# A value step one unit later, and cached keys prepared during the projection before: the attention of a two-layer decoder step on one core

## The chip, the core and the metric

The kernel runs on one core of a Trainium2 chip. Its time is the device time of one execution, in microseconds. The core has five engines that run on their own and wait for each other by semaphores: TensorE (PE, matmuls and transposes by matmul; the loading of its weights is shown apart as PEld), VectorE (DVE), ScalarE (ACT), GpSimd (POOL) and SyncE (SP). SP, ACT and POOL issue DMA transfers, each from its own queue, in the order of its program.

## The reference: what is computed

One inference step of a decoder with two layers, for a prompt of 512 tokens and for 8 single tokens, each with a cache of 128 keys and values. All is in float32. In outline, with D_MODEL 1024, 16 heads of 64, 4 key/value heads, D_FF 2816:

```python
x = x + 0.5 * swiglu(rms(x))            # layer 0
x = x + pool_mixer(rms(x))
x = x + 0.5 * swiglu(rms(x))
k, v = split(rms(x) @ w_kv); k = rope(k)      # one shared K and V
x = x + 0.5 * swiglu(rms(x))            # layer 1, the "down projection" ends this
q = rope(rms(x) @ w_q)
s = q k^T / 8, masked to a causal window of 128
m = maximum(max(s), sink); p = exp(s - m)
o = (p / (sum(p) + exp(sink - m))) @ v
x = x + o @ w_o
x = x + 0.5 * swiglu(rms(x))
y = rms(x)
```

For a single token the keys are its 127 latest cached keys and the new one, and the values likewise. Further outputs are the last 128 keys and values and the last rows of the pooling mixer.

## The kernel before

**Layout and precision.** The residual stream lies transposed in eight tiles `x[k]` of 128 channels by 520 tokens (512 of the prompt, 8 single). A float32 product is made of three fast matmuls: each operand is split into a rounded part and the rest (`split`, lines 238 to 246: ACT copies the rounded part, L242; DVE subtracts, L243), and hi x hi, lo x hi and hi x lo are summed (`terms`, `mm`). Weights are split in the same way by `Weights._split` (L191 on ACT, L192 on DVE).

**Weights.** The class `Weights` streams weight chunks from memory to `raw` buffers (three of 1 MB) on SP's queue and keeps five split pieces ahead of their use. A chunk's load waits until the pieces of the chunk that had its buffer are split. `later` keeps these issues in the order in which they are written. The order of the other instructions on each engine is made by a scheduler when the program is built; pools of buffers (`raw`, `S`, `xh`, `tl`, four PSUM pairs of banks by `duo` and `ps`) decide what has to wait for what.

**Down projection.** `ffn(2, ...)` is the feed-forward half step ahead of the attention. Its last part computes eight tiles, each with matmuls at L410, an eviction by DVE into `u` and an addition to `x[m]` (L589, L590), and then `deferred`, which makes the next layer's split input. A generator given as `before_last` is advanced once per tile.

**Attention.** The queries are eight tiles of two heads. `q_part(t, h)` does one half of tile `t` (24 matmuls at L410), `q_evac` its rotary embedding and split. A unit is a query tile and two of the four blocks of 128 tokens, so there are 16 units. A unit goes through

- `scores` (twelve matmuls, L1004 to L1006),
- `softmax` (mask and maximum on DVE, L1019; exponentials on ACT, L1034; scaling by the sum, half on ACT, L1040, half on DVE, L1042),
- `turn` (transposes by PE, L1052, then `split`),
- `values` (twelve matmuls, L1075, and two copies to `oT` on ACT, L1087).

The loop at line 1211 runs over iterations n: scores of unit n, turn of unit n - 2 (`LAG`), query halves, jobs, softmax of unit n, values of unit n - 2.

**Single tokens.** `turn_keys(b)` transposes the cached keys of token b in iterations 0 to 7 (L1120, copied back by L1121). `sample_scores` (L1127) runs in iterations 10 and 11, `sample_softmax` in 11, `sample_values` (L1159) in 13, all sixteen matmuls at a stretch; the profile shows each of them as two. The caches come on ACT's queue (L950, L953), and the new keys and values are written over row 0 of them by POOL's queue (L951, L954).

**Output projection.** `o_part(m, k0)` adds four of eight input tiles to output tile `m`. The first halves run in iterations 12 to 17 as `jobs`, the second ones after the loop.

Of the kernel before, what the change touches and what calls it, by code (L numbers as in the profile page):

```python
# [18 lines left out]
P = 128  # L19
# [8 lines left out]
PARTS = (8, 8, 6)  # L28
LAG = 2
NPL = (3, 2, 2, 2)  # L30
HD = 64
# [178 lines left out]
def yoco_step(ctx, tc, ins, outs):  # L210
# [651 lines left out]
    with ff_pool() as tmp:  # L862
# [47 lines left out]
        def outputs():  # L910
# [21 lines left out]
            nc.gpsimd.dma_start(v_win_s[:, 127].rearrange("b g d -> b (g d)"), vnew)  # L932

        step = lambda: next(steps, None)
# [6 lines left out]
    with tc.tile_pool(name="at", bufs=2) as at:  # L941
        cst = at.tile([P, 512], F32, name="cst", bufs=1)
        nc.scalar.dma_start(cst, consts[:, C_MASK : C_MASK + 512])
        cosq, sinq = pair(XX, [P, TOK], F32)
        nc.scalar.dma_start(cosq, consts[:, C_COS : C_COS + TOK])
        nc.scalar.dma_start(sinq, consts[:, C_SIN : C_SIN + TOK])
# [3 lines left out]
        nc.scalar.dma_start(kc, cache_k.rearrange("b s g d -> s b (g d)"))  # L950
        nc.gpsimd.dma_start(kc[0:1], knew)  # L951
        for i in range(4):
            nc.scalar.dma_start(vc[i], cache_v[2 * i : 2 * i + 2].rearrange("b s g d -> s b (g d)"))  # L953
            nc.gpsimd.dma_start(vc[i][0:1], vnew[2 * i : 2 * i + 2, :])  # L954

# [3 lines left out]
        oT = [big.tile([P, SP], F32, tag="th", name="oT") for t in range(KT)]  # L959
        kk, vv = [], []  # L960
        for g in range(2):
            kk.append(pair(("tl", "tl"), [P, SP]))
            split(kk[g], kT[g][:, :SP])
        for b2 in range(2):
            vv.append(pair(("tl", "tl"), [P, 2, 256]))
            split(vv[b2], vtok[:, 2 * b2 : 2 * b2 + 2, :])

        def q_half(banks, k0):
# [138 lines left out]
        qq[0] = q_evac(0, qb[0])  # L1107
        q_parts = {1: [(3, 0), (3, 1)]}
        q_evacs = {0: 1, 1: 2, 2: 3}
# [5 lines left out]

        def turn_keys(b):

            pk = ps()
            for g in range(2):
                T.transpose(pk[:, g * P : (g + 1) * P], kc[:, b, g * P : (g + 1) * P], ident)  # L1120
            S.copy(kc[:, b, :], pk[:, :256])  # L1121

        def sample_scores(pd, bs):
            for b in bs:
                for g in range(2):
                    c0 = b * 16 + g * 8
                    T.matmul(  # L1127
                        pd[:, 0, c0 : c0 + 8],
                        kc[:, b, g * P : (g + 1) * P],
                        qz[:, g, :, :, b],  # L1130
                        start=True,
                        stop=True,
                    )

        def sample_softmax(pd):

            sT = at.tile([P, P], F32, name="sT", bufs=1)
            V.tensor_copy(sT, pd[:, 0, :P])
            T.transpose(pd[:, 1, :P], sT, ident)
            smx = at.tile([P, 4], F32, name="smx", bufs=1)  # L1140
            pr = at.tile([P, P], F32, name="pr", bufs=1)
            V.tensor_reduce(smx[:, 0:1], pd[:, 1, :P], axis=AX.X, op=ALU.max)
            V.scalar_tensor_tensor(smx[:, 1:2], smx[:, 0:1], -1.0, sink_s[:, 1:2], op0=ALU.mult, op1=ALU.min)
            S.activation(pr, pd[:, 1, :P], AF.Exp, bias=smx[:, 1:2], accum_out=smx[:, 2:3])
# [6 lines left out]
        def sample_values(pd, pr, bs):  # L1151
            if bs[0] == 0:
                T.transpose(pd[:, 0, :P], pr, ident)
                V.tensor_copy(prT, pd[:, 0, :P])
            pO = pd[:, 1, :P]
            for b in bs:
                for g in range(2):
                    c0 = b * 16 + g * 8
                    T.matmul(  # L1159
                        pO[:, c0 : c0 + 8],  # L1160
                        vc[b // 2][:, b % 2, g * P : (g + 1) * P],
                        prT[:, c0 : c0 + 8],
                        start=True,
                        stop=True,
                    )
            if bs[-1] < NS - 1:
                return
            pO5 = pO.rearrange("p (b t e i) -> p e t i b", b=NS, t=2, e=2)
            for e in range(2):
                rows = slice(e * 64, e * 64 + 64)  # L1170
                for g in range(2):
                    V.tensor_copy(oS[rows, g * 4 : g * 4 + 4, :], pO5[rows, e, g, :, :])

# [11 lines left out]
        def o_part(m, k0, halves_=(0, 1), after=None):  # L1185
# [12 lines left out]

        pd_s, pd_v = [], []
# [121 lines left out]
```

## Time and profile before

| | |
|---|---|
| median of 3 runs | 1728.08 us (1722.71 to 1731.19) |
| profiled execution | 1729.8 us |
| its span, first to last instruction | 1728.0 us |
| instructions | 34367 |
| PE busy | 1669.6 us, 97% |
| DVE busy | 1269.1 us, 73% |
| ACT busy | 904.7 us, 52% |
| mean granted PE clock | 0.980 |

The span is one profiled execution, the time around it is 1.8 us. "Busy" is the time in which an engine executes; matmuls overlap in the array, so a busy PE need not be at its peak. PEclk is the clock that PE was granted, as a share of the full one. In rows of instructions, `out<-in` are the program's tile names, and what stands behind an arrow is the instruction that ended a wait.

### The profile page before, as it was taken

What the parts mean: (1) busy time and instruction counts of PE and PEld (TensorE: products, weight loads), DVE (VectorE), ACT (ScalarE), POOL (GpSimd) and SP (SyncE); (2) the same over time, 40 slices, a digit from 0 to 9 for tenths busy, and PEclk for the clock granted to TensorE, in tenths of its full rate; (3) what the DMA queues carried; (4) which work ended last, traced back from release to release, by engine and by line L of the source; (5) the groups of instructions that cost most, each with busy time, mean ns of one, the idle gap of its engine ahead of it and who ended that gap; (6) DMA issues with size and microseconds to landing.
All of it is one profiled execution on the core that took longest, in us unless ns stands there. A gap on an engine that the chain in (4) does not pass through costs nothing.

```text
span 1728.0 us, 34367 instructions
## 1 busy us (share of the span) xinstructions
PE 1669.6 (97%) x13701; PEld 1654.0 (96%) x13701; DVE 1269.1 (73%) x2454; ACT 904.7 (52%) x1810; POOL 146.1 (8%) x178
## 2 busy tenths in 40 slices
PE   7999999999899999999999999998889999999996
PEld 7999999999899999999999999998779899999996
DVE  6966866877875875887866866878756785785765
ACT  6643634656552643655543634647855653462553
POOL 0101101001001101001101101100000110110100
PEclk9999999999999999999999999999979999999998
DMA  8646746663445845546646746642112465666531
GB/s 204 159 129 141 171 135 144 180 183 75 102 141 132 182 134 135 141 128 145 155 127 141 174 135 141 155 140 50 25 35 73 111 163 144 146 150 159 135 86 51
DMA packets 315872, 227.06 MB, mean 131 GB/s; under 512 B 9265, under 2 KB 290969, under 8 KB 315671
## 3 DMA queue, kind: packets, MB, share of 16 engines
q1 hardware_dynamic: 285872, 174.82, 35.5%
q0 software_dynamic: 23200, 41.82, 14.7%
q10 hardware_dynamic: 6638, 8.23, 1.5%
q8 instruction: 107, 1.75, 0.4%
q14 instruction: 55, 0.44, 0.1%
HBM read 180.89 MB, written 5.04 MB: 108 GB/s over the span
## 4 chain that ended last, share of the span: by engine, by line
PE 67%; DVE 4%; ACT 3%; issue 0%; ACTq 0%; DVEq 0%
PE ps L435 35%; PE ps L410 30%; ACT sm L1034 1%; DVE sm L1019 1%; PE ps L1075 1%; DVE wl L192 1%; PE ps L1159 0%; PE ps L1052 0%; DVE xl L243 0%; ACT xh L242 0%; PE ps L1127 0%; DVE rp L856 0%; ACT wh L191 0%; PE ps L1250 0%; ACT oT L1087 0%
## 5 line engine op out<-in xcount | busy, mean ns | idle before, releaser
L191 ACT ACTIVATE wh<-raw 128x512 fp32r<-128x512 f32 (+1 forms) x742 | 449.6, 621 | 542.8 <-PE ps L410 326.3
L192 DVE TENSOR_TENSOR wl<-raw,wh 128x512 fp32r<-128x512 f32 (+1 forms) x742 | 491.0, 677 | 206.9 <-ACT wh L191 202.2
L435 PE MATMUL ps<-th,wh 128*128 128x260 f32 x1264 | 358.4, 284 | 5.4 <-ACT th L242 3.7
L435 PE MATMUL ps<-tl,wh 128*128 128x260 f32 x1264 | 358.7, 284 | 0.4 <-DVE tl L243 0.4
L435 PE MATMUL ps<-th,wl 128*128 128x260 f32 x1264 | 356.5, 283 | 0.6 <-DVE wl L192 0.5
L410 PE MATMUL ps<-hh,wh 128*128 128x260 f32 x1376 | 282.1, 286 | 4.0 <-DVE mx L1019 3.0
L410 PE MATMUL ps<-hl,wh 128*128 128x260 f32 x1376 | 280.9, 284 | 0.0
L410 PE MATMUL ps<-hh,wl 128*128 128x260 f32 x1376 | 279.4, 283 | 0.0
L435 PEld LDWEIGHTS ps<-th,wh 128*128 128x128 f32 x1264 | 238.9, 189 | 6.7 <-ACT th L242 4.1
L435 PEld LDWEIGHTS ps<-tl,wh 128*128 128x128 f32 x1264 | 239.4, 189 | 1.3 <-DVE tl L243 1.3
L435 PEld LDWEIGHTS ps<-th,wl 128*128 128x128 f32 x1264 | 238.6, 189 | 1.0 <-DVE wl L192 1.0
L410 PEld LDWEIGHTS ps<-hh,wh 128*128 128x128 f32 x1376 | 213.4, 190 | 5.4 <-DVE mx L1019 3.6
L410 PEld LDWEIGHTS ps<-hl,wh 128*128 128x128 f32 x1376 | 215.0, 190 | 0.0
L410 PEld LDWEIGHTS ps<-hh,wl 128*128 128x128 f32 x1376 | 214.0, 189 | 0.0
L435 PE MATMUL ps<-xh,wh 128*128 128x260 f32 x708 | 198.9, 283 | 0.6 <-ACT wh L191 0.6
L435 PE MATMUL ps<-xl,wh 128*128 128x260 f32 x708 | 198.6, 283 | 0.0
L435 PE MATMUL ps<-xh,wl 128*128 128x260 f32 x708 | 194.7, 282 | 1.0 <-DVE wl L192 1.0
L156 POOL DMA_DIRECT2D raw<-raw x79 | 68.4, 866 | 1389.1 <-DVE wl L192 504.7
L589 DVE TENSOR_TENSOR u<-ps,R 128x520 f32<-128x520 f32 x96 | 67.0, 698 | 107.5 <-PE ps L410 107.5
L435 PEld LDWEIGHTS ps<-xh,wh 128*128 128x128 f32 x708 | 133.6, 189 | 1.0 <-ACT wh L191 0.8
L435 PEld LDWEIGHTS ps<-xl,wh 128*128 128x128 f32 x708 | 133.5, 189 | 0.0
L435 PEld LDWEIGHTS ps<-xh,wl 128*128 128x128 f32 x708 | 131.4, 189 | 1.4 <-DVE wl L192 1.4
(237 smaller groups left out, 2845.7 us busy)
## 6 DMA issues: line engine op xcount, KB each, us to landing
raw<-in_ffn_w_gate_dram SPq DMA_DIRECT2D x87, 512.0 KB, 4.1
raw<-in_ffn_w_up_dram SPq DMA_DIRECT2D x87, 512.0 KB, 5.4
raw<-in_ffn_w_down_dram SPq DMA_DIRECT2D x32, 1024.0 KB, 4.9
raw<-raw POOLq DMA_DIRECT2D x79, 256.0 KB, 3.3
S<-in_ffn_w_up_dram SPq DMA_DIRECT2D x79, 256.0 KB, 5.5
S<-raw POOLq DMA_DIRECT2D x79, 256.0 KB, 4.6
raw<-in_ffn_w_down_dram SPq DMA_DIRECT2D x16, 768.0 KB, 6.2
raw<-in_w_q_dram SPq DMA_DIRECT2D x8, 512.0 KB, 6.7
```

What stands on the lines that cost most here:

```text
L156: G.dma_start(blk(raw, 2, 1), blk(raw, 1, 1), accum_op=ALU.add)
L191: nc.scalar.activation(dh, src, AF.Copy)
L192: nc.vector.tensor_tensor(dl, src, dh.bitcast(F32), op=ALU.subtract)
L410: T.matmul(banks[:, hf, :H], a[:, kk, :], hcols(b, hf), start=(first and i == 0), stop=(last and i == 2),)
L435: T.matmul(bank[:, :H], a[:, kk, :], b, start=(not more and kk == 0 and i == 0), stop=(kk == 3 and i == 2), skip_group_check=more,)
L589: V.tensor_tensor(halves(u), banks[m][:, :, :H], halves(R), op=ALU.mult)
L1019: V.tensor_tensor_reduce(out=sm[:, e * 256 : (e + 1) * 256], in0=self.pe[e][:, bi * 256 : (bi + 1) * 256], in1=cst[:, mk : mk + 256], op0= ...
L1034: S.activation(part(i), part(i), AF.Exp, bias=nm[:, i : i + 1], accum_out=den[:, i : i + 1])
L1075: T.matmul(po[:, bi * 256 : (bi + 1) * 256], a, p_[:, kc_], start=(n == 0), stop=(n == 3 * len(kts) - 1),)
```

## The change

The value matmuls of a unit come three iterations behind its scores (`VLAG = 3`); the turning stays two behind. The splits of keys and values, the loads of the cached keys and their transposes are written into a generator that is advanced during the last part of the down projection; the cached keys lie in four `S` buffers instead of one `raw` buffer. The tables of the rotary embedding move from two `xh`/`xl` buffers to one `raw` buffer. The cached values are loaded after iteration 4, on SP's queue and into a `raw` buffer. The query halves of tile 3 are put in iterations 0 and 1 instead of both in 1. The single-token scores are cut into four jobs of four matmuls in iterations 8 to 11, the values into two of eight in iterations 12 and 13, each with a PSUM buffer of its own that is evicted at once, and the first halves of the output projection are dealt out anew over iterations 12 to 18.

```diff
+VLAG = 3
...
+        def attention_prep():
+            for i in range(4):
+                kc.append(splp.tile([P, 2, 256], F32, tag="S", name="kc", bufs=4))
+                later(nc.sync.dma_start(kc[i], cache_k[2 * i : 2 * i + 2].rearrange("b s g d -> s b (g d)")))
+                nc.gpsimd.dma_start(kc[i][0:1], knew[2 * i : 2 * i + 2, :])
+            yield
+            for i in range(4):
+                z = pair(("tl", "tl"), [P, SP])
+                if i < 2:
+                    kk.append(z)
+                    split(z, kT[i][:, :SP])
+                else:
+                    vv.append(tuple(a.rearrange("p (b c) -> p b c", b=2) for a in z))
+                    split(vv[-1], vtok[:, 2 * i - 4 : 2 * i - 2, :])
+                if i:
+                    yield
+            for i in range(4):
+                pk = ps()
+                for j in range(4):
+                    T.transpose(pk[:, j * P : (j + 1) * P], kc[i][:, j // 2, (j % 2) * P : (j % 2 + 1) * P], ident)
+                S.copy(kc[i].rearrange("p b c -> p (b c)"), pk)
+                yield
...
-        ffn(2, tmp, mov3, hooks, tt, XX, deferred(4, tmp, "g", HH, mov4))
+        ffn(2, tmp, mov3, hooks, tt, XX, deferred(4, tmp, "g", HH, mov4), attention_prep())
...
-        cosq, sinq = pair(XX, [P, TOK], F32)
...
-        kc = rawp.tile([P, NS, 256], F32, tag="raw", name="kc")
-        vc = [splp.tile([P, 2, 256], F32, tag="S", name="vc", bufs=4) for _ in range(4)]
...
+        csq = rawp.tile([P, 2, TOK], F32, tag="raw", name="csq")
+        nc.scalar.dma_start(csq.rearrange("p a t -> p (a t)"), consts[:, C_COS : C_COS + 2 * TOK])
...
-        q_parts = {1: [(3, 0), (3, 1)]}
+        q_parts = {0: [(3, 0)], 1: [(3, 1)]}
...
+        def sample_scores(g, b0):
             pk = ps()
+            for b in range(b0, b0 + 4):
+                c0 = (b - b0) * 8
+                T.matmul(
+                    pk[:, c0 : c0 + 8], kc[b // 2][:, b % 2, g * P : (g + 1) * P], qz[:, g, :, :, b], start=True, stop=True
+                )
+            V.tensor_copy(sT4[:, g, b0 : b0 + 4, :], pk[:, :32].rearrange("p (b i) -> p b i", b=4))
...
+        def load_values():
+            vc.append(rawp.tile([P, NS, 256], F32, tag="raw", name="vc"))
+            later(nc.sync.dma_start(vc[0], cache_v.rearrange("b s g d -> s b (g d)")))
+            nc.gpsimd.dma_start(vc[0][0:1], vnew)
+
         jobs = {
-            10: [lambda: pd_s.append(duo()), lambda: sample_scores(pd_s[0], range(0, 4))],
-            11: [lambda: sample_scores(pd_s[0], range(4, 8)), lambda: pd_s.append(sample_softmax(pd_s[0]))],
-            12: [lambda: o_part(0, 0, (0,)), lambda: o_part(1, 0, (0,))],
-            13: [lambda: pd_v.append(duo()), lambda: sample_values(pd_v[0], pd_s[1], range(8))],
+            8: [lambda: sample_scores(0, 0)],
+            9: [lambda: sample_scores(0, 4)],
+            10: [lambda: sample_scores(1, 0)],
+            11: [lambda: sample_scores(1, 4), lambda: pr_s.append(sample_softmax())],
+            12: [lambda: o_part(0, 0, (0,)), lambda: sample_turn(pr_s[0]), lambda: sample_values(0)],
+            13: [lambda: o_part(1, 0, (0,)), lambda: sample_values(4)],
             14: [lambda: o_part(0, 0, (1,)), lambda: o_part(1, 0, (1,))],
             15: [lambda: o_part(2, 0), lambda: o_part(3, 0)],
             16: [lambda: o_part(4, 0), lambda: o_part(5, 0)],
-            17: [lambda: o_part(6, 0), lambda: o_part(7, 0)],
+            17: [lambda: o_part(6, 0)],
+            18: [lambda: o_part(7, 0)],
         }
...
-        for n in range(2 * KT + LAG):
+        for n in range(2 * KT + VLAG):
             if n < 2 * KT:
                 units[n].scores()
-            if n >= LAG:
+            if LAG <= n < 2 * KT + LAG:
                 units[n - LAG].turn()
...
-            if n < NS:
-                turn_keys(n)
-            if n >= LAG:
-                units[n - LAG].values()
+            if n >= VLAG:
+                units[n - VLAG].values()
...
+            if n == 4:
+                load_values()
             if n >= 11:
-                while len(mov5) < (n - LAG + 1) // 2:
+                while len(mov5) < (n - VLAG + 1) // 2:
                     o_split()
```

More of the change, by code (lines that the diff above doesn't have):

```diff
@@ L959, in yoco_step @@
         oT = [big.tile([P, SP], F32, tag="th", name="oT") for t in range(KT)]
[L960 to L966, printed above, removed]
         def q_half(banks, k0):
@@ L1114, in yoco_step, with sample_softmax @@
         prT = at.tile([P, P], F32, name="prT", bufs=1)
-        def turn_keys(b):
+        sT = at.tile([P, P], F32, name="sT", bufs=1)
+        sT4 = sT.rearrange("p (b g i) -> p g b i", b=NS, g=2)
+        def sample_scores(g, b0):
             pk = ps()
[L1119 to L1139, printed above, removed]
+            for b in range(b0, b0 + 4):
[4 more added lines that the diff above has]
+            V.tensor_copy(sT4[:, g, b0 : b0 + 4, :], pk[:, :32].rearrange("p (b i) -> p b i", b=4))
+        def sample_softmax():
+            pd = ps()
+            T.transpose(pd[:, :P], sT, ident)
             smx = at.tile([P, 4], F32, name="smx", bufs=1)
             pr = at.tile([P, P], F32, name="pr", bufs=1)
-            V.tensor_reduce(smx[:, 0:1], pd[:, 1, :P], axis=AX.X, op=ALU.max)
+            V.tensor_reduce(smx[:, 0:1], pd[:, :P], axis=AX.X, op=ALU.max)
             V.scalar_tensor_tensor(smx[:, 1:2], smx[:, 0:1], -1.0, sink_s[:, 1:2], op0=ALU.mult, op1=ALU.min)
-            S.activation(pr, pd[:, 1, :P], AF.Exp, bias=smx[:, 1:2], accum_out=smx[:, 2:3])
+            S.activation(pr, pd[:, :P], AF.Exp, bias=smx[:, 1:2], accum_out=smx[:, 2:3])
             S.activation(smx[:, 3:4], sink_s[:, 0:1], AF.Exp, bias=smx[:, 1:2])
@@ L1149, in sample_softmax, with sample_turn, sample_values @@
             return pr
[L1151 to L1156, printed above, removed]
+        def sample_turn(pr):
+            pk = ps()
+            T.transpose(pk[:, :P], pr, ident)
+            V.tensor_copy(prT, pk[:, :P])
+        def sample_values(b0):
+            pk = ps()
+            for b in range(b0, b0 + 4):
                 for g in range(2):
@@ L1165, in sample_values @@
                     )
-            if bs[-1] < NS - 1:
-                return
-            pO5 = pO.rearrange("p (b t e i) -> p e t i b", b=NS, t=2, e=2)
+            pO5 = pk[:, :64].rearrange("p (b t e i) -> p e t i b", b=4, t=2, e=2)
             for e in range(2):
```

17 lines of the change are left out of this document (6 added, 11 removed).

## Prediction

> **What bounds the kernel now.** First the page: the span, the engines, the clock by slices.
>
> ```profile
> span 1728.0 us, 34367 instructions
> ...
> PE 1669.6 (97%) x13701; PEld 1654.0 (96%) x13701; DVE 1269.1 (73%) x2454; ACT 904.7 (52%) x1810; POOL 146.1 (8%) x178
> ...
> PEclk9999999999999999999999999999979999999998
> ```
>
> PE (TensorE) is busy 97% of the span, so only a stage where it idles or runs slowly can give time back. Apart from the ends the clock falls in one slice of the forty, 1253 to 1296 us: the attention. So I asked for the busy times in stretches there, cut where the clock changes.
>
> ```profile
> core 0: us, PE busy (x) PEld busy (x) DVE busy (x) ACT busy (x) POOL busy (x), PEclk, DMA share, GB/s
> 1126.00:1152.00 26.00, 26.00 (x220) 26.00 (x219) 23.98 (x41) 16.28 (x28) 0.00 (x0) 1.00 0.41 115
> ...
> 1211.30:1225.90 14.60, 12.97 (x113) 11.91 (x111) 11.82 (x43) 11.84 (x36) 0.00 (x0) 1.00 0.09 27
> ...
> 1240.60:1244.90 4.30, 2.83 (x25) 2.19 (x24) 4.30 (x17) 2.58 (x10) 0.00 (x0) 0.98 0.01 2
> 1244.90:1265.20 20.30, 18.82 (x93) 17.48 (x94) 11.77 (x50) 12.34 (x40) 0.00 (x0) 0.50 0.22 52
> 1265.20:1275.20 10.00, 8.15 (x67) 7.05 (x66) 5.17 (x20) 6.63 (x21) 0.00 (x0) 1.00 0.01 2
> 1275.20:1285.50 10.30, 10.30 (x55) 9.85 (x54) 2.88 (x16) 4.97 (x20) 0.00 (x0) 0.51 0.00 0
> 1285.50:1291.00 5.50, 3.91 (x32) 3.57 (x30) 3.92 (x17) 3.07 (x12) 0.00 (x0) 0.98 0.00 0
> ...
> 1296.00:1342.00 46.00, 46.00 (x389) 46.00 (x388) 30.39 (x53) 26.49 (x55) 0.92 (x1) 1.00 0.32 85
> ```
>
> Four stages. The **down projection** (1126 to 1152) keeps PE full. In the **query phase** (to 1240.6; its middle pair of units is the second row) PE is 89% busy, VectorE (DVE) and ScalarE (ACT) 81% each. The **bare units** 10 to 14 (1240.6 to 1291) have hardly any query work beside them: PE runs 30.6 us of these 50.4 at half clock. The **tail** (1296 to 1342, output projection) is full again. The timeline of PE shows the bare units: the first score matmuls of units 10, 12, 13 and 15 (L1004), the end of unit 10's scores (L1052 follows), and the two blocks of single-token matmuls.
>
> ```profile
> 1240.58 0.39 PE L1004 MATMUL ps<-tl,xh 64*128 64x256 f32 x2
> ...
> 1241.50 0.44 PE L1052 MATMUL ps<-ident,sm 128*128 128x128 f32 x2
> ...
> 1247.13 4.70 PE L1127 MATMUL ps<-qz,kc 128*128 128x8 f32 x22
> ...
> 1260.89 0.59 PE L1004 MATMUL ps<-tl,xh 64*128 64x256 f32 x2
> ...
> 1271.24 0.39 PE L1004 MATMUL ps<-tl,xh 64*128 64x256 f32 x2
> ...
> 1274.89 6.29 PE L1159 MATMUL ps<-prT,vc 128*128 128x8 f32 x32
> ...
> 1290.97 0.40 PE L1004 MATMUL ps<-tl,xh 64*128 64x256 f32 x2
> ```
>
> Both slow stretches begin within 2.3 us of these blocks. Five units take 50.4 us, 10.1 each, against 7.3 in the query phase, which has more work. Then the waits from 1140 to 1325:
>
> ```profile
> PE ps L1075 <- ACT xh L242: 7.4, 7, 1.6
> ...
> PE ps L1052 <- DVE sm L1042: 2.1, 1, 2.1
> ```
>
> PE's largest wait, 7.4 us, is that of the value matmuls (L1075) for the split of the turned weights on ACT (L242), which the same iteration has only just asked for. That is what a later value step removes.
>
> **Part A: keys turned in the down projection.** The transposes and copies of the cached keys, and from the chain of waits what projection matmuls and transposes take of PE when it is full, and when the queries' norm (L378) begins:
>
> ```profile
> L1120 PE MATMUL ps<-ident,kc x16: 272/272/328, 1171.3 to 1224.4; 128*128 128x128 f32 x16
> ...
> L1121 ACT COPY kc<-ps x8: 349/370/374, 1171.8 to 1225.3; 128x256 f32<-128x256 f32 x8
> ```
> ```profile
> 1157.35 1.01 PE ps L378 x10
> ...
> 1303.29 2.87 PE ps L410 x24
> 1306.16 0.44 PE ps L1052 x4
> ```
>
> A matmul takes 2.87/24 = 0.12 us, four transposes 0.44. The built program's order puts the 16 key transposes, four at a time, among the last tiles of the down projection, where PE is full: 4 x 0.44 = +1.8 us. In the attention they cost as much, but the query phase has PE slack, so I credit nothing there. The eight ACT copies (8 x 0.37 = 3.0 us) leave the query phase; four larger ones go where ACT is busy 16.3 of 26 us. Each time a PSUM pair is borrowed from the four that the projection turns over, with DVE 92% busy there; a late eviction could cost some tenths.
>
> The transposes wait for the key loads on SP's queue and for the new key, patched in by POOL's queue. The loads stand behind a query chunk (first row); the second row has the time to landing of the value cache's loads and patches, whose shape they have.
>
> ```profile
> 1123.95 0.99 SPq L256 DMA_DIRECT2D raw<-in_w_q_dram  x2
> ```
> ```profile
> DMA to landing us min/median/max: 2.7/6.8/8.2
> ```
>
> The first key lands at about 1125 + 8.2 and its patch 2.7 later: 1136. In the built order the first transposes stand 78 pairs of matmuls ahead of L378: 78 x 2 x 0.12 = 18.7 before 1157.35, at 1138.7. That spares 2.7 us; if it is missed, all that is queued on PE stands. A: +1.8, between +1.8 and +5.
>
> **Part B: splits, tables, later values, in the query phase.**
>
> ```profile
> L243 DVE TENSOR_TENSOR tl<-kT,tl x2: 686/686/687, 1111.3 to 1112.5; 128x512 fp32r<-128x512 f32 x2
> ...
> L243 DVE TENSOR_TENSOR tl<-vtok,tl x2: 682/688/694, 1120.7 to 1121.6; 128x512 fp32r<-128x512 f32 x2
> ```
>
> The key and value splits already run at 1111 to 1122, ahead of the down projection, although they are written after it, and the built order leaves them there: 0. That part of the change doesn't do what it says.
>
> ```profile
> 1158.53 0.39 ACTq L950 DMA_DIRECT2D kc<-in_cache_k_win_dram  x1
> ```
> ```profile
> 1223.03 2.04 SPq L256 DMA_DIRECT2D raw<-in_w_o_dram  x2
> 1256.24 1.25 SPq L256 DMA_DIRECT2D raw<-in_w_o_dram  x2
> ```
>
> The tables' load takes the place on ACT's queue that the key load had (1158.5), half its size, for a use some 8 us on: 0. The value cache goes to SP's queue in unit 4, into a weight buffer. Behind it stand the third and fourth output chunks, which went out at 1223 and 1256; they now wait for the tables' last use (unit 9, about 1241) and the last single-token values (unit 13, about 1275). With 8.2 us to land they are there at 1283, and what they feed is the second half of the output projection, in the tail: 0.
>
> Later values take out PE's wait for ACT. But in the query phase PE is one limit of three: of the 2.8 us that DVE idles in a pair of units I take 1 for each of three pairs, -3. Against it stands the opening. In DVE's built order rotary steps, a split and the maxima of unit 2 go ahead of unit 0's scaling; some seven operations at about 0.69 (the splits' row) put the first scaled tile 5 us later. PE idled 2.1 us there (second wait above); it would now idle about 7, but DVE, which is never idle there, makes most of it up: +2. B: -1, between -5 and +5.
>
> **Part C: the bare units.** What a unit needs on ACT: four exponentials (first row, of the chain), two scalings, two splits, two copies.
>
> ```profile
> 1242.32 2.08 ACT sm L1034 x8
> ```
> ```profile
> L1040 ACT ACTIVATE sm<-sm,den 128x256 f32<-128x256 f32 x32 | 14.5, 501 | 0.6 <-DVE den L1037 0.5
> L242 ACT ACTIVATE xh<-ps 128x512 fp32r<-128x512 f32 x24 | 14.3, 594 | 7.4 <-PE ps L1052 7.1
> L1087 ACT COPY oT<-ps 64x256 f32<-64x256 f32 x32 | 11.6, 363 | 7.3 <-PE ps L1075 6.9
> ```
>
> 2.08 + 2 x 0.50 + 2 x 0.59 + 2 x 0.36 = 5.0 us, 25 for five. DVE: its five stretches from 1240.6 sum to 28.0. PE: scores 0.9 (1240.58 to 1241.50), twelve value matmuls 1.4, eight transposes 0.9, so 3.2 a unit and 16.0 for five; two projection halves of two tiles, 48 x 0.12 = 5.7; and the single tokens. These took 4.70/22 and 6.29/32, about 0.2 us each, at half clock; at full clock between 0.1 and 0.2, and I take 0.11, for 48 of them 5.3. PE 27.0. So two engines need 27 to 28 us. DVE got to 81% in the query phase: 28/0.8 = 35 us. With the single tokens cut into pieces of 8 and 16 matmuls (as the profile counts them) I expect the slow clock for a quarter of PE's work: 6.8 us more, of which a third shows: 37.3. The extra lag leaves one more unit's values for the tail (1.4). C: 37.3 + 1.4 - 50.4 = -11.7. Ends: DVE at 90%, 31.1 + 1.4 - 50.4 = -18; all of PE's work at half clock, 54 + 1.4 - 50.4 = +5.
>
> The Trainium skill (TensorE: Matmul & The Clock Gate, Part 1) lets the clock halve after an idle window of about 3.4 us and return after a busy one. The trace agrees only in part: at 1244.9 the clock fell after 4.3 us in which PE was busy 2.83. By that rule alone no stretch in the new order would be slow, and C would be an estimate of -14.
>
> The tail keeps its matmuls; the last values, their copy and split stand behind three quarters of a projection tile: 0, at most +2.
>
> **Sum.** 1.8 - 1 - 11.7 = -10.9. The profiled execution took 1729.8 us (1728.0 of span and 1.8 around it), so 1718.9; the median of the three runs, 1728.1, is 1.7 lower: **1717**.
>
> **Rivals.** *Larger gain* (0.17): no slow clock, DVE at 90%, the opening free: 1.8 - 3 - 18 = -19, 1709. For it: the slow stretches began at the blocks of single tokens, and the blocks are gone. Against: the bare units still have little for PE. *Hidden* (0.14): the chain of scores, maximum, exponential, scaling, turning sets the spacing, not PE. Unit 12 to 13 took 10.3 us with more than half at full clock. If five units keep 9.2 us each (46 + 1.4 - 50.4 = -3), the sum is -2: 1726. *Slower* (0.21): the clock. Single-token pieces now stand in all of units 8 to 13; if each drags the clock down, the bare units run at half throughout: C +5, A +1.8, B 0: about +7, 1735. The gain is gone once 20 of PE's 27 us run at half clock (27 + 20 = 47 = 50.4 - 1.4 - 1.8, rounded). For it: the clock fell at 1244.9 with little idle before. Against it: it was back at 1265.2, with the first projection half, which comes no later now.
>
> **Chances.** This kernel can be told from no change beyond 0.5%, 8.6 us. The forecast has 0.48; of its own span, 1711 to 1724, three quarters of the chance lie below 1719.4: 0.36. With the larger gain faster is 0.53; same 0.12 + 0.14 = 0.26; slower 0.21. The range 1706 to 1734 leaves out about half of the slower case and a tail of the larger gain.
>
> **What would show it.** In the profile after: kT and vtok split before 1126; PE's wait for ACT xh under 2 us; key transposes in the down projection with no wait for a patch; units 10 to 15 in 33 to 41 us with under 15 us at half clock; a PE gap of 5 us or more before unit 0's transposes. Wrong if the bare units keep over 46 us, if PE stands for a key patch, or if the query phase's pairs take over 15.5 us.

## The result

The changed kernel takes 1719.7 us (median; 1717.4 to 1720.6) against 1728.1 us before: a ratio of 0.9947, 95% interval 0.9932 to 0.9963. That is 8.4 us, 0.5% faster, just past what can be told from no change (by the ratio, which compares runs on the same chip, 9.2 us). The profiled execution took 1718.4 us, 1716.7 of it span; before it was 1729.8 and 1728.0. The trace of before shows one of that kernel's longer executions and the trace of after one of its shorter ones, so the two traces differ by 11.4 us, 3 more than the medians.

The page, in the lines shown of before:

```profile
span 1716.7 us, 34378 instructions
...
PE 1657.4 (97%) x13701; PEld 1643.2 (96%) x13701; DVE 1268.5 (74%) x2461; ACT 904.8 (53%) x1806; POOL 146.2 (9%) x178
...
PEclk9999999999999999999999999998999999999998
```

PE has the same 13,701 matmuls, 12.2 us less busy time and the same share: it ran them faster, and the clock's dip in the attention went from a 7 to an 8. The stretches of the attention, cut at the first scores of units 0, 10 and 15 and at the next norm, first before and then after:

```profile
1170.98:1240.58 69.60, 60.24 (x503) 55.16 (x502) 59.60 (x211) 56.36 (x163) 0.00 (x0) 0.98 0.20 46
1240.58:1290.97 50.39, 44.01 (x264) 40.12 (x263) 28.02 (x116) 29.56 (x100) 0.00 (x0) 0.70 0.09 22
1290.97:1348.73 57.76, 56.73 (x476) 56.10 (x476) 39.40 (x75) 33.24 (x67) 2.69 (x3) 1.00 0.36 92
```

```profile
core 0: us, PE busy (x) PEld busy (x) DVE busy (x) ACT busy (x) POOL busy (x), PEclk, DMA share, GB/s
1174.38:1244.66 70.28, 60.66 (x501) 55.97 (x501) 59.38 (x211) 52.98 (x153) 0.51 (x1) 0.93 0.18 46
1244.66:1284.16 39.50, 32.71 (x251) 29.13 (x251) 27.89 (x118) 27.69 (x91) 0.00 (x0) 0.91 0.23 54
1284.16:1340.52 56.36, 54.98 (x466) 54.61 (x465) 39.08 (x78) 35.63 (x78) 2.69 (x3) 1.00 0.38 94
```

The bare units (the second row of each) take 39.5 us instead of 50.4. PE is at half clock for about 7 us of them: (1 - 0.91) x 2 x 39.5; finer windows give 6.8, and 30.7 before. PE's waits from 1140 to 1325:

```profile
PE ps L1064 <- DVE sm L1054: 7.2, 1, 7.2
PE ps L1135 <- DVE qz L993: 3.3, 1, 3.3
PE ps L411 <- ACT oT L1099: 3.2, 5, 1.4
PE ps L1064 <- DVE xl L244: 3.2, 5, 1.1
PE ps L1016 <- ACT xh L243: 1.0, 1, 1.0
```

The value matmuls (now L1087) no longer wait for ACT; that was 7.4 us. The opening's wait for unit 0's first scaled tile went from 2.1 to 7.2, and there is a wait that the prediction didn't have: the third piece of the single tokens' scores stands 3.3 us for the query columns (`qz`) of tile 7. On PE's timeline, with unit 10's first scores ahead of it and the second piece of the single tokens' values behind it:

```profile
1244.66 0.39 PE L1016 MATMUL ps<-tl,xh 64*128 64x256 f32 x2
...
1250.45 1.06 PE L1135 MATMUL ps<-qz,kc 128*128 128x8 f32 x8 [3.30 <-DVE qz L993]
...
1272.56 1.85 PE L1165 MATMUL ps<-prT,vc 128*128 128x8 f32 x16
```

### The profile page after: what moved, and what is told of

Its sections match the earlier page's. It is cut to its first block, busy times and chain, and to the rows that moved or that the text cites. A ratio compares the mean times of both kernels' runs of the same rounds, so it can differ in the third digit from the quotient of the medians.

```text
span 1716.7 us, 34378 instructions
## 1 busy us (share of the span) xinstructions
PE 1657.4 (97%) x13701; PEld 1643.2 (96%) x13701; DVE 1268.5 (74%) x2461; ACT 904.8 (53%) x1806; POOL 146.2 (9%) x178
## 3 DMA queue, kind: packets, MB, share of 16 engines
q8 instruction: 107, 1.75, 0.4%
## 4 chain that ended last, share of the span: by engine, by line
PE 68%; ACT 3%; DVE 3%; issue 0%; ACTq 0%; DVEq 0%
PE ps L436 35%; PE ps L411 31%; PE ps L1087 1%; ACT sm L1046 1%; PE ps L1064 0%; DVE wl L193 0%; DVE xl L244 0%; DVE sm L1031 0%; PE ps L379 0%; ACT wh L192 0%; ACT xh L243 0%; PE ps L1263 0%; ACT oT L1099 0%; DVE tl L244 0%; ACT th L243 0%
```

## The experiments

**Question.** The comparison of the two traces suggests this theory: single tokens in pieces keep the clock up in the bare units, and that is the gain. The rival: the later values are the gain, by the waits that they take out. A third part, the early key transposes, might help or harm either. The parts were undone one at a time, and the later values also done alone. The new tables and the value load on SP's queue were not undone alone.

All kernels in one table. The stage columns are from the profiled execution: first norm to unit 0's scores, to unit 10's, to unit 15's, to the next norm, in us, cut as above. "Half" is the time at half clock between units 10 and 15, "idle" that in which PE stands there. "Gain" is 1728 x (1 - ratio) in us; an interval of the ratio is some 2 us wide to each side, up to 4. The stages are of one execution each, and differences of one or two us between them can come without any edit: up to the first norm the traces of before and of e13, whose code is the same there, take 1157.2 and 1158.5 us, and those of e2 and e1 1158.7 and 1160.9.

| kernel | to u0 | u0-u10 | u10-u15 | to norm | half | idle | ratio (95%) | gain |
|---|---|---|---|---|---|---|---|---|
| before | 13.8 | 69.6 | 50.4 | 57.8 | 30.7 | 6.4 | 1 | 0 |
| after | 14.9 | 70.3 | 39.5 | 56.4 | 6.8 | 6.8 | 0.9947 (0.9932-0.9963) | 9.2 |
| e1_lag2 | 14.9 | 77.1 | 39.1 | 59.2 | 7.8 | 7.3 | 0.9999 (0.9988-1.001) | 0.2 |
| e2_blocks | 14.9 | 68.5 | 47.5 | 56.0 | 23.9 | 7.0 | 0.9983 (0.9968-0.9997) | 2.9 |
| e4_keysback | 13.8 | 70.8 | 38.4 | 56.4 | 6.8 | 5.8 | 0.993 (0.9907-0.9954) | 12.1 |
| e12_lag2_keys | 13.8 | 76.2 | 35.6 | 57.6 | 6.8 | 3.9 | 0.9957 (0.9941-0.9973) | 7.4 |
| e13_before_lag3 | 13.8 | 68.9 | 46.2 | 55.6 | 27.3 | 3.8 | 0.9948 (0.9934-0.9962) | 9.0 |
| e5_filler | 13.8 | 69.6 | 49.9 | 56.7 | 17.1 | 5.1 | 1.0012 (0.9999-1.0026) | -2.1 |
| e6_qz | 14.9 | 69.1 | 35.4 | 55.2 | 6.8 | 3.5 | 0.9921 (0.9904-0.9937) | 13.7 |
| e7_q2 | 12.7 | 70.1 | 39.5 | 56.4 | 13.7 | 4.3 | 0.9933 (0.9918-0.9948) | 11.6 |
| e8_gapfill | 14.9 | 71.3 | 36.3 | 56.4 | 5.9 | 5.0 | 0.9949 (0.993-0.9969) | 8.8 |
| e9_keys_qz | 13.8 | 70.7 | 35.2 | 56.4 | 6.8 | 2.9 | 0.9903 (0.9883-0.9924) | 16.8 |
| e10_keys_qz_q2 | 12.7 | 74.1 | 36.8 | 55.2 | 6.8 | 4.6 | 0.9928 (0.9909-0.9947) | 12.4 |
| e11_keys_qz_fill | 13.8 | 70.0 | 35.5 | 56.3 | 6.8 | 3.5 | 0.989 (0.987-0.991) | 19.0 |

### Values at a lag of two again

```diff
-VLAG = 3
+VLAG = 2
-            17: [lambda: o_part(6, 0)],
-            18: [lambda: o_part(7, 0)],
+            17: [lambda: o_part(6, 0), lambda: o_part(7, 0)],
```

> The changed kernel with the values again two units behind the scores; single tokens in pieces and the early key transposes stay. If the later values carry a good part of the gain, PE's wait for ACT's split of the turned weights comes back (about 7 us in all), a pair of units in the query phase takes 14.5 to 15 us instead of 13.1, units 10 to 15 take 43 to 46 us instead of 39.5, and the time is about 1726. If the pieces of single tokens (through the clock) carry it alone, the query pairs stay near 13.1 and units 10 to 15 near 39.5, and the time is within 2 us of the changed kernel's 1719.7.

The whole gain is gone: 1727.7 us. But not where it was expected. The windows, first scores to unit 10 and unit 10 to 15, and one of PE's waits:

```profile
1175.75:1252.89 77.14, 62.95 (x503) 57.71 (x503) 61.92 (x214) 53.84 (x154) 0.51 (x1) 0.91 0.17 42
1252.89:1292.03 39.14, 31.86 (x246) 28.83 (x246) 28.03 (x120) 29.75 (x100) 0.00 (x0) 0.90 0.24 55
```
```profile
PE ps L1087 <- ACT xh L243: 8.0, 5, 3.4
```

The wait for ACT is back, 8.0 us; the bare units keep their 39 us, and 6.9 us are lost between units 0 and 10 and 2.8 behind unit 15. The opening's gap is the same 7.2 us. Of the 6.9 us, 2.4 are lost by unit 4 (31.4 us after the first scores instead of 29.0), just ahead of which PE's longest wait for ACT stands; the rest is lost between units 4 and 10, where 1.1 us of that wait, 2.2 of waits for DVE's maxima and 5.4 us at half clock lie. So the bare units stay short without the later values, but the gain in time does not come without them.

### Single tokens in blocks again

```diff
-            8: [lambda: sample_scores(0, 0)],
-            9: [lambda: sample_scores(0, 4)],
-            10: [lambda: sample_scores(1, 0)],
-            11: [lambda: sample_scores(1, 4), lambda: pr_s.append(sample_softmax())],
-            12: [lambda: o_part(0, 0, (0,)), lambda: sample_turn(pr_s[0]), lambda: sample_values(0)],
-            13: [lambda: o_part(1, 0, (0,)), lambda: sample_values(4)],
+            10: [lambda: sample_scores(0, 0), lambda: sample_scores(1, 0)],
+            11: [lambda: sample_scores(0, 4), lambda: sample_scores(1, 4), lambda: pr_s.append(sample_softmax())],
+            12: [lambda: o_part(0, 0, (0,)), lambda: o_part(1, 0, (0,))],
+            13: [lambda: sample_turn(pr_s[0]), lambda: sample_values(0), lambda: sample_values(4)],
```

> The changed kernel with the single-token matmuls again in blocks (scores of both key groups in iterations 10 and 11, all values in 13, none beside output projection halves); values three units behind and early key transposes stay. If the blocks drop the clock, PE runs 17 to 30 us at half clock between units 10 and 15 (6.8 in the changed kernel), these units take 45 to 50 us, and the time is 1725 to 1730. If the later values alone carry the gain, half clock may come but units 10 to 15 stay at 39 to 42 us and the time within 2 us of 1719.7.

```profile
1173.59:1242.12 68.53, 59.03 (x481) 54.11 (x481) 58.17 (x208) 52.47 (x152) 0.51 (x1) 0.93 0.19 47
1242.12:1289.62 47.50, 40.51 (x268) 37.48 (x267) 28.67 (x123) 29.79 (x99) 0.00 (x0) 0.75 0.20 46
```

The clock falls as expected, 23.9 us at half, and the bare units take 47.5 us: 8.0 more, of which the clock is 7.6, half of the 15.3 us more that PE is busy at half clock. The time, 1723.2 us, is less than was expected; 1.8 us come back ahead of unit 10, where the first pieces no longer stand. Pieces instead of blocks are worth 3.4 us of the 8.4 in this kernel by the medians and 6.3 of the 9.2 by the ratios, not all of it.

### Keys transposed in the attention again

```diff
-            for i in range(4):
-                pk = ps()
-                for j in range(4):
-                    T.transpose(pk[:, j * P : (j + 1) * P], kc[i][:, j // 2, (j % 2) * P : (j % 2 + 1) * P], ident)
-                S.copy(kc[i].rearrange("p b c -> p (b c)"), pk)
-                yield
...
+            if n < NS:
+                turn_keys(n)
```

> The changed kernel with the cached keys loaded as there, but transposed and copied in iterations 0 to 7 of the attention, one token each. If the transposes cost their time in the down projection and are free among the query phase's PE slack, the queries' norm starts 1.8 to 2.3 us earlier (at about 1157.5) and the end is as much earlier: about 1717.7. If the eight copies on ACT and the transposes cost the same in the query phase (a pair of units 13.7 instead of 13.1), the time is equal, within 1 us of 1719.7. If moving them was a gain, it is 1721 or more.

None of the numbers was right: it is 1715.3 us, 4.4 better than the changed kernel by the medians and 2.9 by the ratios, whose intervals overlap; the four executions (1714.4 to 1716.3) all lie below the changed kernel's seven (1717.4 to 1720.6). The chain of the down projection, with the keys there (the changed kernel) and without (this one):

```profile
1121.75 17.56 PE ps L411 x147
1139.30 0.44 PE ps L958 x4
1139.74 4.30 PE ps L411 x36
...
1153.96 5.73 PE ps L411 x48
1159.69 1.01 PE ps L379 x10
```
```profile
1121.96 36.19 PE ps L411 x303
1158.16 1.01 PE ps L379 x10
```

The four groups cost what was reckoned: 4 x 0.44 = 1.76 us, and the stretch takes 37.94 us (1121.75 to 1159.69) against 36.19 for the same 303 matmuls, 1.75 more. The other part comes behind: 1.0 us before unit 0, where PE's wait for ACT (L1016, 1.0) is gone, and 1.1 us in the bare units; units 0 to 10 take 0.5 more with the keys among them.

### The later values alone, and everything but them

The kernel before with the lag of the values as its only edit, and the changed kernel with a lag of two and late keys:

```diff
+VLAG = 3
-            17: [lambda: o_part(6, 0), lambda: o_part(7, 0)],
+            17: [lambda: o_part(6, 0)],
+            18: [lambda: o_part(7, 0)],
-            if n >= LAG:
-                units[n - LAG].values()
+            if n >= VLAG:
+                units[n - VLAG].values()
-                while len(mov5) < (n - LAG + 1) // 2:
+                while len(mov5) < (n - VLAG + 1) // 2:
```

> The kernel before with the values three units behind the scores and nothing else (the last output job one iteration later). If the later values are worth 8.0 us by themselves, as undoing them in the changed kernel cost, the stretch from the first scores to unit 10 falls from 69.6 to about 63 us and the time is about 1720. If they are worth only PE's waits for ACT that other engines don't make up (7.4 us in all, a third to a half of it), it is 1724 to 1726. If they are only needed in the changed kernel, to take up its longer opening, the time is 1727 to 1729; units 10 to 15 keep 30 us at half clock in each case.

> The changed kernel with the values two units behind and the keys transposed in iterations 0 to 7, so that of its parts the pieces of single tokens, the tables, the query order and the value load on SP's queue remain. If the costs and gains add (lag 8.0, early keys 4.4 us), it takes 1727.7 - 4.4 = 1723. If a lag of two costs so much only because it cannot take up the opening's gap, and the gap shrinks with the keys' move (7.2 to 5.6 us), it is 1719 to 1721.

The later values alone bring 9.0 us (1718.3): as much as the whole change. The rest without them and without early keys brings 7.4 (1721.0): the second of its two cases by the time, while the opening with its later stages to unit 10 still takes 76.2 us. The windows of the first, and two of its waits:

```profile
1172.28:1241.16 68.88, 62.56 (x502) 56.67 (x501) 59.73 (x213) 55.23 (x162) 0.00 (x0) 0.95 0.20 47
1241.16:1287.36 46.20, 42.45 (x264) 39.04 (x263) 27.20 (x114) 29.46 (x99) 0.00 (x0) 0.70 0.10 24
```
```profile
PE ps L1053 <- DVE sm L1043: 2.0, 1, 2.0
...
PE ps L1076 <- ACT xh L243: 0.3, 1, 0.3
```

The time of the kernel before with later values is that of the first case, but the stretch to unit 10 is not: it is 0.7 us shorter, not 6.6. PE's wait for ACT falls from 7.4 to 0.3 us; before, 4.0 us of it lay ahead of unit 10 and 3.4 in the bare units, of which 1.6 just before unit 15. The bare units are 4.2 us shorter (2.6 of it PE's idle time, 1.4 the clock), with the clock nearly as low as before, and the stretch behind unit 15 is 2.2 shorter. These stages sum to 7.1 us; another 3.0 us of the difference of the two traces lie behind the second norm, where the code is the same.

### Filling PE with matmuls that nothing reads

To see what the slow clock itself costs, wide matmuls were added: in the kernel before three written behind each single token, and in the changed kernel 48 in the opening's gap.

```diff
+        def fill():
+            pf = ps()
+            vh = vv[0][0]
+            for i in range(3):
+                T.matmul(pf[:, :256], vh[:, 0, :P], vh[:, 1, :], start=True, stop=True)
```

> The kernel before, with 48 more matmuls of 256 columns that nothing reads (three after each token's single-token matmuls in iterations 10, 11 and 13), 5.8 us of work more for PE at full clock. If what drops the clock is that PE streams few columns there, the half-clock time between units 10 and 15 falls from 30.7 to under 15 us and these units take 44 to 48 us instead of 50.4 in spite of the added work, the time 1722 to 1726. If the clock does not matter for the spacing of the units, or more work does not lift it, they take 51 to 56 us and the time is 1729 to 1734.

```diff
+            if n == LAG:
+                pf = ps()
+                for i in range(48):
+                    T.matmul(pf[:, :256], vv[0][0][:, 0, :P], vv[0][0][:, 1, :], start=True, stop=True)
```

> The changed kernel with 48 matmuls of 256 columns that nothing reads, put on PE's queue between unit 2's scores and unit 0's transposes, where PE stands for 7.2 us (5.2 us of work at full clock). If idling there is what halves the clock for the next 10.2 us, the half clock falls to 3.4 us or less, unit 4's scores come 3 to 5 us earlier, and the time is 1715 to 1717. If DVE paces the opening, the clock stays up but unit 4 comes within 1 us of 29.0 us after the first scores, and the time is 1719 to 1721. If the clock falls for another reason, half clock stays near 10 us and the time is 1720 or more.

The first did not interleave as written. In the built order the sixteen value matmuls still stand at a stretch, with the wide ones behind them; on PE's timeline:

```profile
1276.43 3.74 PE L1166 MATMUL ps<-prT,vc 128*128 128x8 f32 x32
```

So it is no test of wide matmuls among the narrow ones. It took the half clock down to 17.1 us, not to under 15, and gained nothing: the bare units took 49.9 us. Against before, the clock takes 6.1 us less of PE's time there (8.5 against 14.6, half of the busy time at half clock) and PE idles 1.3 us less, but it has 6.9 us more work (36.3 against 29.4, reckoned at full clock). The second did its work in the opening, which shows in the windows: almost no half clock (0.99 against 0.93 from unit 0 to 10).

```profile
1174.89:1246.21 71.32, 64.97 (x549) 59.74 (x549) 62.30 (x219) 53.13 (x152) 0.51 (x1) 0.99 0.21 55
1246.21:1282.46 36.25, 31.21 (x252) 28.37 (x251) 24.86 (x110) 27.56 (x91) 0.00 (x0) 0.92 0.18 40
```

Unit 4 came 25.9 us after the first scores instead of 29.0, and unit 10 nonetheless 71.3 us after them, not 70.3. DVE is busy 62.3 of these 71.3 us. So taking the half clock out of the opening this way (10.2 us there in the changed kernel) brought nothing that lasts to unit 10. PE was busy for only 5.9 of the 10.2 us, so there were 2.9 us to win, and it now has 6.8 us more work in the stretch; the time, 1717.9 us, cannot be told from the changed kernel's.

### The two new waits

```diff
-            10: [lambda: sample_scores(1, 0)],
-            11: [lambda: sample_scores(1, 4), lambda: pr_s.append(sample_softmax())],
+            11: [lambda: sample_scores(1, 0), lambda: sample_scores(1, 4), lambda: pr_s.append(sample_softmax())],
```

> The changed kernel with the single tokens' scores of the second key group moved from iteration 10 to 11 (two pieces of four there), so that PE need not stand for tile 7's query copy behind DVE's maxima. If that wait (3.3 us of PE at 1247) and the 3.4 us of half clock after it are lost time, units 10 to 15 take 35 to 37 us instead of 39.5 and the time is 1715 to 1717. If DVE sets the pace there and the wait only moves to the next transposes, they take 39 to 40 us and the time is 1719 to 1721.

The first theory holds: the bare units fall to 35.4 us and the time to 1714.5, better than was expected.

```profile
1244.44:1279.83 35.39, 31.94 (x247) 28.53 (x247) 27.25 (x116) 26.80 (x89) 0.00 (x0) 0.90 0.26 60
```

```diff
-        for h in (0, 1):
-            q_part(2, h)
         qq[0] = q_evac(0, qb[0])
-        q_parts = {0: [(3, 0)], 1: [(3, 1)]}
+        q_parts = {0: [(2, 0), (2, 1)], 1: [(3, 0), (3, 1)]}
```

> The changed kernel with the third query tile's two projection halves moved from ahead of unit 0 into iteration 0, and the fourth's into iteration 1; its rotary steps thereby leave DVE's queue ahead of unit 0's scaling. If the order on DVE makes the opening longer, PE's gap before unit 0's transposes falls from 7.2 us to under 4, the stretch from the first scores to unit 4's falls from 29.0 to 24 to 27 us, and the time is 1715 to 1718. If the rotary steps are only late elsewhere, unit 4 waits for its query tile, the stretch stays at 28 to 31 us, and the time is 1719 to 1722.

```profile
PE ps L1016 <- ACT xh L243: 4.7, 1, 4.7
...
PE ps L1064 <- DVE sm L1054: 0.6, 1, 0.6
```

The gap is gone (0.6 us), but without tile 2's matmuls PE stands 4.7 us ahead of the first scores. Unit 4 comes 26.4 us after the first scores, as was expected of the first case, but unit 10 no earlier (70.1 us). The time is 1715.8 us, 2.4 below the changed kernel by the ratios, whose intervals overlap; the stages show 2.1 of it, unit 0's scores counted from the norm.

### The edits together

> The changed kernel with two of its parts put otherwise: the cached keys are transposed in iterations 0 to 7 again, and the single tokens' scores of the second key group come in iteration 11. If the two costs are separate, their gains add, 4.4 and 5.3 us from 1719.7: about 1710. If both fill the same slack of PE around units 8 to 11, the time is that of the better one, 1713 to 1715.

> The same with the third query tile's projection in iteration 0 and the fourth's in iteration 1 as well. If the order of DVE in the opening is a cost of its own, 2 to 4 us come off the kernel with the other two edits: 1706 to 1709. If the earlier first scores only meet a wait for the query split of tile 0 (4.7 us when this edit stood alone) and the gap is made up by DVE, the time is within 1.5 us of the kernel with the two.

> Keys in iterations 0 to 7 and the second group's scores in iteration 11, with 36 matmuls of 256 columns that nothing reads between unit 2's scores and unit 0's transposes. If half clock in the opening costs half of its time, 3.4 us come off the kernel with the two edits (its opening half clock is expected at 6.8 us): 1706 to 1708. If DVE makes up for it by unit 10, as when the filler stood alone, the time is within 1.5 us of the kernel with the two.

The late keys and the scores in iteration 11 together: 1711.9 us. The gains add in the main (16.8 us against 12.1 and 13.7 alone; 2.9 + 4.5 on top of 9.2 would be 16.6). Tile 2's later projection on top takes 4.7 us away again (1716.6), which was neither of its two cases: units 0 to 10 take 74.1 us. The filler on top gives the fastest kernel of the study, 1709.9 us, a ratio of 0.989 (0.987 to 0.991) to before, but its 2 us over the kernel without it lie between its two cases and within the intervals.

## Why the prediction was right, and where it was not

The forecast was 1717 and faster; it is 1719.7 and faster, and the make-up is only in part the one that was forecast. Most of what it said would show is there: the splits of kT and vtok before 1126, the new keys on POOL's queue by 1135.4 and the first key transposes at 1139.1 without a wait, a gap of 7.2 us before unit 0's transposes, and units 10 to 15 in 39.5 us with 6.8 us at half clock. The first rows for the keys:

```profile
L958 PE MATMUL ps<-ident,kc x16: 270/272/273, 1139.1 to 1153.7; 128*128 128x128 f32 x16
L942 SPq DMA_DIRECT2D kc<-in_cache_k_win_dram x4: 469/524/2172, 1125.6 to 1128.9; - x4
L943 POOL DMA_DIRECT2D kc<-knew x4: 497/516/540, 1132.6 to 1134.9; - x4
```

By its own steps, with the two profiled executions:

**A, +1.8.** In the down projection exactly that, 1.75 us, and no eviction was late. The step that failed is "I credit nothing there" for the query phase: with the keys back in the attention the kernel is 7.2 us faster with a lag of two (7.4 against 0.2, beyond the intervals) and 2.9 with a lag of three (12.1 against 9.2, within them). A belongs at +3 to +7. The transposes cost 0.5 us between units 0 and 10; part of what they cost elsewhere is the 1.0 us wait ahead of unit 0. Why the bare units too are shorter with late keys is open.

**B, -1.** From the norm to unit 10 the sum is +1.7: 85.1 us against 83.4. The gap was right (7.2), its cost of +2 can't be told apart from the other parts: unit 4 comes 3.7 us later after the first scores than before (29.0 against 25.3), unit 10 only 0.7. The -3 for later values is mis-sized twice. Done alone, they bring 0.7 us there: 4.0 of the 7.4 us of waiting lay ahead of unit 10, and PE idles 3.0 us less, but it runs 3.4 us longer at half clock, which takes 1.6 back, and has 0.7 more work. Undone in the changed kernel they cost 6.9 there: PE idles 4.6 us more and runs 3.4 longer at half clock, which takes 1.6. The step took one number for both kernels. Why the same edit is worth so much more there, and how much of that the longer opening explains (2.4 us by unit 4), is open.

**C, -11.7.** Units 10 to 15 were to take 37.3 us, -13.1, and take 39.5, -10.9. The +1.4 for the last unit's values in the tail was wrong in sign: the stretch behind unit 15 is 1.4 shorter. PE has 1.75 us less work in it (54.98 against 56.73 us busy, 466 records against 476) and idles 1.4 us instead of 1.0. The whole is -12.3. That this is close to -11.7 is partly luck: the tail makes up for a stretch that took 2.2 us longer than forecast. A stretch's length can be split into PE's work reckoned at full clock, half of the time that PE is busy at half clock, and PE's idle time. Before: 29.4 + 14.6 + 6.4 = 50.4; after: 29.3 + 3.4 + 6.8 = 39.5; with the wait for `qz` removed 28.7 + 3.3 + 3.5 = 35.4, rounded. So in these units the gain is the clock (11.2 us), at the same work and slightly more idle time.

The prediction had DVE at 80% as the base, 35 us, and 2.3 for the clock; it wrote 6.8 us of loss and counted a third. Measured are 6.8 us at half clock and 3.4 of loss, and that this loss shows in full is borne out by the blocks put back (7.6 us more of it, 8.0 us longer), but it is no rule: with tile 2's projection later, these units run 13.7 us at half clock and still take 39.5, with 4.3 us idle. What was left out is the wait for `qz`. DVE's timeline of the changed kernel has tile 7's last rotary step (L859) and its query columns (L993) behind the four maxima of unit 10 (L1031):

```profile
1247.15 0.41 DVE L1031 CUSTOM_DVE_ANT_0 sm<-ps,cst 128x256 f32<-128x256 f32 x1
...
1248.60 0.69 DVE L859 TENSOR_TENSOR qT<-qT,rp 128x520 f32<-128x520 f32 x1
...
1249.98 0.15 DVE L993 COPY qz<-qT 64x8 f32<-64x8 f32 x1
...
1250.23 0.17 DVE L993 COPY qz<-qT 64x8 f32<-64x8 f32 x1
```

The piece of single-token scores in iteration 10 is at the head of PE's queue by 1247.2 and can start only after them. The prediction priced the piece and did not ask when its operand is ready. It also read the slow stretches as beginning at the blocks of single tokens. The first begins at 1244.8 in the trace of before, 2.4 us ahead of its block (1247.13), so that block did not start it; the blocks can only have kept it up.

**The attribution** was wrong in its weights. In the bare units the clock is what changed, as C said, but C gave the pieces 13 us and B gave the later values 3. The later values alone give 9.0 us, as much as the whole change, with the half clock of the bare units hardly lower (27.3 us against 30.7), and the pieces (with the new tables, query order and value load) give 7.4 alone and 3.1 on top of the later values (12.1 - 9.0). That the two take partly the same time is likely but not shown: alone they sum to 16.4 us by the ratios and 14.0 by the medians, against 12.1 together, and each figure has an interval of 2 to 4 us to each side. The early keys then take some 3 us away. By stages the sum is 1.75 + 1.7 - 12.3 = -8.9 us against the -10.9 forecast. That the total came near is luck in part: the later values were put too low, the pieces too high, and the two errors offset.

**Outside the sum.** The span behind the second norm is 376.1 us against 379.3. In other kernels it lies between 375.5 and 379.9, without order by edit; 1.7 us of the difference is the slow clock at the restart of the next feed-forward step (3.4 us at half clock before, none after). It is no part of the change that any run here shows.

**The rivals.** "Slower" asked for half clock in all bare units; with pieces it is 6.8 us, and 13.7 at most. "Hidden" asked for five units in 46 us; that is what the later values alone look like (46.2), and it came with 9 us of gain, not 2: the stretch behind unit 15 was shorter too, and so was the span behind the second norm. "Larger gain", 1709 us, was reached only with two parts put otherwise and a filler (1709.9).

## What to carry to other kernels

When a change has several parts, undo each and do each alone: here the part that was credited with 3 us brings as much alone as the whole change (9.0 us), and a third part takes some of the gain away. Before moving a small job ahead, look up when its last operand leaves its engine's queue, not only when its data were computed before; one piece placed an iteration too early cost PE 3.3 us of waiting, and with that removed the stretch is 4.1 us shorter. On the full engine the moved transposes cost their time exactly (4 x 0.44 us), and leaving them at the old place was cheaper, so what a move saves there has to be looked up, not put at nothing. And look at the built order before reading a filler's result: the scheduler had put the wide matmuls behind the block that they were written into.

## What the runs showed of the hardware

The slow clock comes in whole windows. In the attention its stretches last 3.4, 20.5 and 10.2 us before, 10.2, 3.4 and 3.4 after, and likewise in every kernel here: multiples of 3.41 us on one grid per run. Rows of the changed kernel, cut on this grid:

```profile
1186.73:1190.14 3.41, 0.00 (x0) 0.00 (x0) 3.12 (x13) 3.29 (x16) 0.00 (x0) 0.50 0.00 0
1190.14:1193.55 3.41, 2.41 (x11) 2.41 (x12) 2.13 (x9) 3.10 (x10) 0.00 (x0) 0.50 0.00 0
...
1244.76:1248.17 3.41, 1.91 (x18) 1.30 (x18) 3.41 (x13) 2.08 (x9) 0.00 (x0) 1.00 0.00 0
1248.17:1251.58 3.41, 1.13 (x10) 1.13 (x11) 3.33 (x15) 3.39 (x13) 0.00 (x0) 1.00 0.80 202
1251.58:1255.00 3.42, 3.42 (x16) 2.97 (x15) 1.59 (x8) 3.14 (x12) 0.00 (x0) 0.51 0.52 105
...
1265.24:1268.65 3.41, 3.23 (x29) 3.24 (x29) 1.24 (x10) 2.65 (x10) 0.00 (x0) 1.00 0.02 5
...
1272.06:1275.48 3.42, 3.20 (x29) 3.00 (x28) 1.86 (x11) 2.59 (x13) 0.00 (x0) 1.00 0.00 0
1275.48:1278.89 3.41, 3.41 (x18) 3.41 (x18) 1.87 (x10) 2.48 (x9) 0.00 (x0) 0.50 0.79 210
1278.89:1282.30 3.41, 3.41 (x31) 2.93 (x31) 1.72 (x9) 0.91 (x2) 0.00 (x0) 1.00 0.46 98
```

In several of these rows a window's clock fits what PE did in the one before: no work, then half clock; 1.13 us of work, then half clock; a full window at half clock, then full clock again. But busy time doesn't decide. The window from 1272.06 has PE busy for 3.20 of 3.42 us, and the next runs at half clock; the one from 1244.76 is busy for 1.91 and keeps the clock. Narrow matmuls as such don't decide either: the windows from 1265.24 and 1272.06 each hold sixteen records of single-token matmuls of 8 columns (1.85 us), and the first keeps the clock. And a window can be busy from end to end and still be followed by half clock, when its work is nearly all such records: in the kernel before at half clock (first row), and in the kernel before with the filler at full clock (second row).

```profile
1248.17:1251.58 3.41, 3.41 (x18) 3.41 (x18) 1.49 (x4) 2.63 (x7) 0.00 (x0) 0.50 0.00 0
1276.42:1279.83 3.41, 3.41 (x34) 3.41 (x32) 1.50 (x5) 3.13 (x12) 0.00 (x0) 1.00 0.00 0
```

The columns that PE streams order the windows better. Summed over the matmul records that start in a window (8 for a single-token record, 256 for a scores record), they are 576 from 1248.2 and 2188 from 1272.1, with half clock next, and 2944 from 1265.3 and 3328 from 1244.8, with full clock next. In the 6,948 windows of all fourteen traces, half clock follows all 142 with under 1,856 columns and full clock all 6,560 with over 4,112; of the 246 in between, 74 are followed by half clock and 172 by full. By busy time both follow anywhere from 1.5 to 3.41 us.

The Trainium skill (TensorE: Matmul & The Clock Gate, Part 1) gives a free-running window of 3413 ns, and the grid agrees. Its idle window as the cause of the fall agrees at 1248 only in part (PE did 1.13 us of work in it) and not at 1272. What exactly the clock counts as activity, and why the windows in between go either way, these runs don't settle.

Fixed windows may also be why the opening's gap of 7.2 us, the same in the changed kernel and in the one with the scores in iteration 11, gives 10.2 us of half clock in one and 6.8 in the other: it would depend on where the grid lies. No run sets the grid on purpose, but the same program run again bears on it. In 62 executions of the kernel before, beside the experiments, the mean granted clock lies between 0.976 and 0.984 and the time between 1733.8 and 1723.1 us; those at 0.983 take 1724.9 us in the mean and those at 0.979 1730.9. An estimate from the two clocks is 0.004 x 1728 x 2 = 14 us more at half clock, and half of that, 6.9 us if PE is busy throughout, is near the 6.0 measured.
